# A hybrid decoder block on one core: splitting recurrent outputs where they are made, and moving attention's small work between ScalarE, VectorE and GpSimd

## The chip, the core and the metric

The kernel runs on one core of a Trainium2 chip. The core has TensorE (PE, matrix products; its weight loads are the row PEld), VectorE (DVE), ScalarE (ACT), GpSimd (POOL) and SyncE (SP, which here issues most of the transfers). The metric is the device time in microseconds (us); lower is better.

## The reference

One layer of a decoder block on a sequence of 2048 positions, 1024 wide, in fp32:

```python
h = rms_norm(x, g_norm[l]) * (1.0 + scale) + shift
x_rnn, z_rnn, q, k, v, z_attn, g_r, g_a = split(h @ w_in[l])
xc = causal_depthwise_conv(x_rnn, conv_w[l], conv_b[l])
hr = rg_lru(xc, ...)                       # gated linear recurrence over the positions
y_rnn = (hr * silu(z_rnn)) @ w_out_rnn[l]
o = dilated_attention_mixture(rope(q), rope(k), v)
y_attn = (o * silu(z_attn)) @ w_out_attn[l]
merged = sigmoid(g_r + bg_r) * y_rnn + sigmoid(g_a + bg_a) * y_attn
x = x + gate * (merged @ w_o[l])           # and a last rms_norm
```

The attention has 8 heads of 128. It mixes three causal windows (128 positions at stride 1, 512 at stride 4, 2048 at stride 16), each position weighted by the three softmax denominators.

## The kernel before

**Products in two parts.** Every fp32 operand of a product is split into a high part `h`, which is the number rounded to the type `fp32r` by a copy, and a low part `l`, the rest. A product is then three matmuls (`mm3`: h·h, h·l, l·h). So each operand costs one copy (`hi_act` on ScalarE, or `hi_dve` on VectorE) and one subtraction (`lo_pool` on GpSimd, or `lo_dve` on VectorE).

**Stages.** The positions are worked on in two halves of 1024, each two blocks of 512 columns.

1. For each half the input projection, by Strassen's scheme for 2x2 blocks: seven products of 12 matmuls (`strassen`), whose left operands are made in the first half (and stored as `sD`) and loaded in the second (tile `S`, seven buffers). Among them runs the recurrence: `recurrent` works on 128 channels and two blocks of 512 positions; its steps (taps, split, gates, decay, root, scan, finish) are hung onto the product counter by `steps_after`, so that each runs some products later. `finish` multiplies the recurrent state by its gate, in the tile `zs` (two buffers), and stores it as `yaT`.
2. Attention, 16 heads (8 of the first half, 8 of the second, which have longer key ranges), together with six output products called jobs: the recurrent output product for four blocks (`yaT`, n = 0 to 3) and the attention output product for the first two (`oT`).
3. The other two attention output products and the last projection.

Stages 1 and 3 are ordered by a scheduler from its own cost model. Attention is not: under `manual_schedule` each engine runs its instructions in the order in which the code issues them.

**Attention's order.** A head is six units (`ORDER`): four of strided keys (`c`, 0 to 3; these serve the two dilated windows) and two of local blocks (`w`, 0 and 1). One unit's scores are computed in each slot, the same unit's transposes `LAG` = 7 slots later and its sums one slot after that. In a slot the places are, in order:

- HEAD: high and low parts of keys and queries (`kq`), evictions of the slot before, then the scores on TensorE (`scores_c`, `scores_w`; tile `sc`, two PSUM banks) and their softmax: VectorE adds the mask and takes the extreme (`softmax_tile`, L986), ScalarE the exponential and its sum (L987). The result is `pp`, the statistics are `st`.
- EXCHANGE, once a head (slot e, six after its first): the matmul `exchange` brings the gathered statistics `sm` of the other windows to each position, into an `sc` bank; `maxima`, `exponentials` and then (WEIGHTS) `weights` turn them into the factors `M`.
- The transposes (L1072, L1085; tile `pT`, two banks) and `split_p`, which makes the high and low parts `pth` and `ptl` of a transposed tile.
- TAIL: `scale`, which multiplies the probabilities of the unit whose transposes come in the next slot by `M`; the split of its values (`vh`, `wh`); loads for later slots; and, at the end of slot e - 1, `gather`, which spreads `st` into `sm`.

Between these places `spend` runs 3.6 steps of the jobs per slot, one step being the three matmuls of one k. A job is 64 steps (8 tiles m by 8 k). Its right operands, `yh` and `yl`, are made in the last eight steps of the job before: `load_y` brings `yraw` (four buffers) at steps 44, 46, 48 and 50 and then at each step from 57 on, and `split_y` makes both parts of one k at each step from 56 on. `NY` is the number of buffers of each.

Before the change the lines that matter are: `scale` (L1046 to L1052: VectorE's `tensor_scalar` for `c` at L1049, ScalarE's `activation` for `w` at L1052), `split_p` (L1057), `gather` (L1136, on GpSimd at L1140), `finish` (L678), `load_y` and `split_y` (L1278 and L1285).

Of the kernel before, what the change touches and what calls it, by code (L numbers as in the profile page):

```python
# [10 lines left out]
F32 = mybir.dt.float32  # L11
# [9 lines left out]
P = 128  # L21
S = 2048
D = 1024
# [61 lines left out]
def decoder_block(ctx, tc, x, c, positions, g_norm, w_mod, b_mod, w_in, b_gate, conv_w, conv_b,  # L85
# [10 lines left out]
    def scratch(name, shape):  # L96
        return nc.dram_tensor(name, shape, F32, kind="Internal").ap()
# [5 lines left out]
    zaT = scratch("zaT", [D, S])  # L103
    grT = scratch("grT", [D, S])
    gaT = scratch("gaT", [D, S])
    yaT = scratch("yaT", [D, S])
    mrT = scratch("mrT", [D, S])
    oT = scratch("oT", [D, S])
    meT = scratch("meT", [D, S])
# [42 lines left out]
    def hi_act(o, i):  # L152
        nc.scalar.activation(o, i, AF.Copy)  # L153
# [442 lines left out]
    def recurrent(rp, bigr, f, m):  # L596
# [25 lines left out]
        def x_part(j, ps, u):  # L622
# [55 lines left out]
            def finish():  # L678
                z4 = zs[j][:].rearrange("p (r j) -> p r j", r=4)
                nc.vector.tensor_tensor(z4, v["y"][:].rearrange("p (j r) -> p r j", r=4), z4, ALU.mult)  # L680
                c0 = f * HALF + j * CH
                nc.sync.dma_start(yaT[m * P : (m + 1) * P, c0 : c0 + CH], zs[j][:])

            if j == 0:
                start[0] = n_prod[0]
            steps_after(start[0] + 7 * j, (
                (0, tap), (1, taps), (2, split), (4, gates), (5, sigmoids), (6, decay), (7, exponentials),
                (8, root), (9, scan), (10, finish)))

        def done(i, j, ps, u):  # L690
            (z_part if i else x_part)(j, ps, u)
# [199 lines left out]
    sc = pools.open("sc", bufs=2, space=PSUM)  # L891
    ap_ = pools.open("ap", bufs=1)
    fl = pools.open("fl", side="right", bufs=1)
    NY = 8

    NW = 4
    msk = T(ap_, [P, N_CST - K_M23], F32, "msk")
# [25 lines left out]
    class Head:  # L923
# [121 lines left out]

        def scale(self, kind, x):  # L1046
            for i, pp in enumerate(self.u[kind, x]):
                if kind == "c":
                    nc.vector.tensor_scalar(pp, pp, self.M[:, 0, x, i : i + 1], None, ALU.mult)  # L1049
                else:  # L1050
                    pp = pp[0][:, pp[1] :]
                    nc.scalar.activation(pp, pp, AF.Copy, scale=self.M[:, 1, i, x : x + 1])  # L1052

        def transposes(self, kind, x):
            (self.transposes_c if kind == "c" else self.transposes_w)(x)

        def split_p(self, pt, cols):  # L1057
            th = T(ap_, [P, CH], F32R, "pth", bufs=4)
            tl = T(ap_, [P, CH], F32R, "ptl", bufs=4)
            hi_act(th[:, cols], pt[:, cols])  # L1060
            lo_dve(tl[:, cols], pt[:, cols], th[:, cols])
            return th, tl

        def transposes_c(self, r):
            pp, out = self.u.pop(("c", r)), []
            for k0 in range(0, self.bk[1] + 1, 2):
                pt = T(pT, [P, CH], F32, "pT")
                w = 2 * P + (P if k0 + 1 == self.bk[1] else 2 * P)
                for k in (k0, k0 + 1):
                    c0 = (k % 2) * 2 * P  # L1070
                    for j, i in enumerate([i for i, n in enumerate(self.bk) if n >= k]):
                        nc.tensor.transpose(pt[:, c0 + j * P : c0 + (j + 1) * P], pp[i][:, k * P : (k + 1) * P], ident)  # L1072
                out.append(self.split_p(pt, slice(0, w)))
            self.u["tc", r] = out

        def transposes_w(self, i):

            pt_, out = self.u.pop(("w", i)), []
            for pieces in ((1, 2, 3, 4), (5, 6, 7, 0)):
                pt = T(pT, [P, CH], F32, "pT")  # L1080
                if self.bk[i] == 0 and 0 in pieces:
                    pieces = pieces[:3]
                for c, x in enumerate(pieces):
                    pp, half = pt_[x // 2][0], x % 2
                    nc.tensor.transpose(pt[:, c * P : (c + 1) * P], pp[:, half * P : (half + 1) * P], ident)  # L1085
                out.append(self.split_p(pt, slice(0, len(pieces) * P)))
            self.u["tw", i] = out


# [46 lines left out]
        def gather(self):  # L1136

            self.sm = T(ap_, [P, 2, 4, 2, 8], F32, "sm")
            for g in range(2):
                nc.gpsimd.tensor_tensor(  # L1140
                    self.sm[:, g], self.st[:, :, g].rearrange("p t b n -> p t (b n)").unsqueeze(1).broadcast_to([P, 4, 2, 8]),
                    qm.unsqueeze(2).unsqueeze(3).broadcast_to([P, 4, 2, 8]), ALU.mult)

# [54 lines left out]
        def enlist(self, B):  # L1198
# [3 lines left out]
            for i, s in enumerate((B, B + 2)):  # L1202
                at(s, HEAD, self.window_queries, i)
            e = B + NU
            at(e - 1, TAIL, self.gather)
            at(e, EXCHANGE, self.exchange)
            at(e, EXCHANGE, self.maxima)
            at(e, EXCHANGE, self.exponentials)
# [58 lines left out]
    def steps(jobs):  # L1267
# [4 lines left out]
        def load_w(x):  # L1272

            if x < 2 * len(tiles):
                j, m = tiles[x // 2]
                W[x] = load_wd(jobs[j][0], m, x % 2)

        def load_y(j, k):  # L1278
            if j < len(jobs):
                w, ys, n = jobs[j]  # L1280
                assert ys is yaT or all((n // 2, h, n % 2) in stored for h in range(H))
                t = raw["y", j, k] = T(fl, [P, CH], F32, "yraw", bufs=4)
# [1 line left out]

        def split_y(j, k):  # L1285
            if j < len(jobs):
                t = raw.pop(("y", j, k))
                yh = T(fl, [P, CH], F32R, "yh", bufs=NY)
                yl = T(fl, [P, CH], F32R, "yl", bufs=NY)
                hi_act(yh[:], t[:])  # L1290
                lo_pool(yl[:], t[:], yh[:])
                Y[j, k] = yh, yl

        def load_g(t):
            j, m = tiles[t]
# [28 lines left out]
        for t, (j, m) in enumerate(tiles):  # L1324
            ps = T(pj, [P, CH], F32, "pj")
            for k in range(KT):
# [15 lines left out]
                step = m * KT + k  # L1342
                if step in range(KT * KT - 20, KT * KT - 12, 2):
                    load_y(j + 1, (step - KT * KT + 20) // 2)
                if step >= KT * KT - KT:
                    if k and k + 3 < KT:
                        load_y(j + 1, k + 3)
                    split_y(j + 1, k)
                yield
            last = ps  # L1350
        evict(len(tiles) - 1, last)
# [129 lines left out]
```

## Time and profile before

| | |
|---|---|
| Median of 3 runs | 2396.19 us (2390.61 to 2397.49) |
| Profiled execution: its own time | 2398.24 us |
| Profiled execution: its span | 2396.5 us |
| Busy share of the span: PE, DVE, ACT, POOL | 94%, 58%, 47%, 43% |
| TensorE clock granted over the span | 0.975 |
| Bytes moved | 577.06 MB, 241 GB/s in the mean |
| Attention in the span | about 1503 to 2105 us |

How to read the profile: a row of groups has the line, the engine, the operation, what it writes and reads (out<-in), the shape and the count; behind the bar the time in which it kept the engine busy, the mean duration of one in ns, and the idle time of the engine just before it with what ended it. A row of stages has the stretch, then the busy time of each engine with its instructions, the granted share of TensorE's clock, the mean busy share of the 16 DMA engines and GB/s. A row of waits names who waited for whom, the total, how often, and the longest.

### The profile page before, as it was taken

The page shows a single profiled execution, that of the slowest core. Times are in us where ns is not written, and L with a number is a line of the kernel's source. Part 1 is how long each engine was busy: PE and PEld are TensorE (multiplying, and loading weights), DVE is VectorE, ACT ScalarE, POOL GpSimd, SP SyncE. Part 2 cuts the span into 40 slices and gives each one's busy share as a digit, 9 for nine tenths or more (in the row PEclk, how much of TensorE's full clock was granted, in tenths as well). Part 3 has the DMA queues.
Part 4 walks back from the last instruction along what each step waited for, and adds up shares of the span by engine and source line. Part 5 has one row for each costly group of instructions (what it writes and reads, how often), then busy time and mean ns, then how long its engine had stood idle before and what let it go on. Part 6 is the DMA issues. An engine that isn't in the chain of part 4 may idle for free.

```text
span 2396.5 us, 34064 instructions
## 1 busy us (share of the span) xinstructions
PE 2245.3 (94%) x11397; PEld 1884.5 (79%) x11397; DVE 1392.2 (58%) x2439; ACT 1137.7 (47%) x2268; POOL 1034.0 (43%) x813
## 2 busy tenths in 40 slices
PE   5899999999989999999999998999989898989998
PEld 5897777777777897878888876888878787878887
DVE  6847666766585734443444561477767787845433
ACT  3436656666542525555444411565666666522211
POOL 2566556665554643332211011456565757342000
PEclk9999999999999999999999998999999999999999
DMA  7266877677778559999666776988887678698752
GB/s 264 85 216 216 277 252 263 234 265 252 245 261 267 164 165 330 314 325 294 211 222 224 263 230 228 282 244 261 262 255 240 215 226 253 211 316 278 234 189 97
DMA packets 416295, 577.06 MB, mean 241 GB/s; under 512 B 71934, under 2 KB 278006, under 8 KB 415096
## 3 DMA queue, kind: packets, MB, share of 16 engines
q1 hardware_dynamic: 378680, 455.33, 60.7%
q10 hardware_dynamic: 37440, 119.55, 13.1%
q8 instruction: 90, 1.47, 0.2%
q14 instruction: 85, 0.70, 0.1%
HBM read 362.95 MB, written 211.82 MB: 240 GB/s over the span
## 4 chain that ended last, share of the span: by engine, by line
PE 55%; DMA 10%; DVE 10%; issue 9%; POOL 7%; ACT 5%; SPq 3%; ACTq 1%; POOLq 0%; DVEq 0%
PE pj L145 42%; PE pq L145 7%; PE pg L145 2%; PE sc L145 1%; PE o L145 1%; POOL S L159 1%; DMA wraw<-in_w_in_dram 1%; POOL yl L159 1%; DVE acc L485 1%; DMA wD<-s 1%; POOL vh L159 1%; POOL kq L159 1%; DMA yraw<-yaT 1%; DMA fg<-mrT 1%; DMA vraw<-vN 1%
## 5 line engine op out<-in xcount | busy, mean ns | idle before, releaser
L145 PE MATMUL pj<-T,S 128*128 128x512 f32 x4704 | 1121.5, 398 | 28.6 <-DVE ev L338 17.3
L145 PEld LDWEIGHTS pj<-T,S 128*128 128x128 f32 x4704 | 890.4, 190 | 248.0 <-DVE ev L338 22.5
L145 PE MATMUL pj<-yh,w 128*128 128x512 f32 x1024 | 373.8, 410 | 10.7 <-ACT yh L153 10.7
L159 POOL TENSOR_TENSOR S<-wraw,S 128x512 fp32r<-128x512 f32 x168 | 240.0, 1441 | 176.0 <-ACT S L186 105.0
L145 PEld LDWEIGHTS pj<-yh,w 128*128 128x128 f32 x1024 | 197.6, 193 | 47.8 <-ACT yh L153 11.8
L987 ACT ACTIVATE pp<-pp,st 128x256 f32<-128x256 f32 (+3 forms) x256 | 133.5, 523 | 171.0 <-DVE st L986 171.0
L145 PE MATMUL pj<-yl,w 128*128 128x512 f32 x512 | 205.3, 401 | 2.6 <-POOL yl L159 2.5
L145 PE MATMUL pj<-S,T 128*128 128x256 f32 x1152 | 161.1, 295 | 11.3 <-POOL S L159 7.9
L162 DVE TENSOR_TENSOR ptl<-pT,pth 128x384 fp32r<-128x384 f32 (+1 forms) x160 | 94.8, 626 | 124.6 <-ACT pth L153 124.4
L145 PEld LDWEIGHTS pj<-S,T 128*128 128x128 f32 x1152 | 150.8, 200 | 13.7 <-POOL S L159 9.4
L159 POOL TENSOR_TENSOR S<-s,S 128x512 fp32r<-128x512 f32 x84 | 114.4, 1362 | 91.5 <-ACT S L186 55.3
L159 POOL TENSOR_TENSOR yl<-yraw,yh 128x512 fp32r<-128x512 f32 x64 | 84.8, 1350 | 125.7 <-DMA yraw<-yaT 63.5
L640 DVE SCALAR_TENSOR_TENSOR xc<-xr,par,xc 128x512 f32<-128x512 f32 x96 | 83.5, 870 | 60.5 <-ACT xc L634 57.4
L1049 DVE TENSOR_SCALAR pp<-pp,M 128x128 f32<-128x128 f32 (+3 forms) x128 | 117.3, 956 | 0.0
L159 POOL TENSOR_TENSOR wh<-vraw,wh 128x640 fp32r<-128x640 f32 (+1 forms) x32 | 48.3, 1510 | 159.2 <-ACT wh L153 135.9
L292 DVE TENSOR_TENSOR u<-pj,u 128x512 f32<-128x512 f32 x56 | 38.4, 685 | 134.7 <-PE pj L145 79.5
L145 PEld LDWEIGHTS pj<-yl,w 128*128 128x128 f32 x512 | 99.1, 194 | 19.0 <-POOL yl L159 5.8
L986 DVE CUSTOM_DVE_ANT_0 pp<-sc,msk 128x256 f32<-128x256 f32 (+3 forms) x256 | 102.7, 444 | 16.1 <-PE sc L145 15.7
L159 POOL TENSOR_TENSOR kq<-kraw,kq 128x512 fp32r<-128x512 f32 (+1 forms) x64 | 102.1, 1607 | 13.8 <-ACT kq L153 13.8
L145 PE MATMUL pq<-oh,mh 128*128 128x512 f32 x256 | 98.6, 394 | 8.9 <-ACT mh L153 8.9
L620 POOL TENSOR_TENSOR zs<-zs,sg 128x512 f32<-128x512 f32 x32 | 46.0, 1437 | 133.1 <-ACT sg L616 132.5
L145 PE MATMUL pq<-ol,mh 128*128 128x512 f32 x256 | 100.7, 393 | 0.0
(287 smaller groups left out, 3996.1 us busy)
## 6 DMA issues: line engine op xcount, KB each, us to landing
sD<-S ACTq DMA_DIRECT2D x196, 512.0 KB, 3.4
S<-sD SPq DMA_DIRECT2D x196, 512.0 KB, 5.3
w<-wD SPq DMA_DIRECT2D x128, 512.0 KB, 5.7
wraw<-in_w_in_dram SPq DMA_DIRECT2D x136, 256.0 KB, 3.4
wD<-s ACTq DMA_DIRECT2D x64, 256.0 KB, 4.0
T<-in_w_mod_dram SPq DMA_DIRECT2D x8, 1024.0 KB, 9.6
vN<-ev SPq DMA_DIRECT2D x64, 128.0 KB, 2.3
zaT<-ev SPq DMA_DIRECT2D x32, 256.0 KB, 3.4
```

The costliest lines, as they stand in the source:

```text
L145: last_mm[0] = nc.tensor.matmul(o, lhsT=l, rhs=r, start=st, stop=sp, **kw).ins
L159: nc.gpsimd.tensor_tensor(o, i, h.bitcast(F32), ALU.subtract)
L162: nc.vector.tensor_tensor(o, i, h.bitcast(F32), ALU.subtract)
L292: nc.vector.tensor_tensor(u2[:], Z[:], u1[:], ALU.add)
L485: nc.vector.scalar_tensor_tensor(acc[:], t[:, k, :], ca[:, k : k + 1], acc[:], ALU.mult, ALU.add)
L620: (2, lambda: nc.gpsimd.tensor_tensor(z[:], z[:], sg[0][:], ALU.mult))))
L640: nc.vector.scalar_tensor_tensor(xc, xr[:, i : i + CH], cw(i), xc, ALU.mult, ALU.add)
L986: nc.vector.tensor_tensor_reduce(pdst, s_ps, mask, 1.0, 3e38, ALU.add, ALU.min, m_)
L987: nc.scalar.activation(pdst, pdst, AF.Exp, bias=m_, scale=-1.0, accum_out=l_)
L1049: nc.vector.tensor_scalar(pp, pp, self.M[:, 0, x, i : i + 1], None, ALU.mult)
```

## The change

- In the second half's recurrence one more step, `halves`, splits the finished output: ScalarE makes the high part `yh`, GpSimd the low part, in place in `zs`. The store comes one step later and is two transfers: the low part to `yaT`, the high part to the new `yhT`.
- The jobs on these two blocks (n = 2 and 3; `in_parts`) load `yh` and `yl` ready, with no `yraw` and no split.
- In the other jobs the low part of odd k goes to VectorE. `NY` grows from 8 to 9, and `split_y` runs one step ahead (its first at step 55).
- In attention ScalarE scales the units `c` as well; the high part of a transposed local block is made by VectorE; and `gather` moves from GpSimd at the end of slot e - 1 to VectorE at the head of slot e, in front of the evictions.

```diff
@@ recurrent
             def finish():
                 z4 = zs[j][:].rearrange("p (r j) -> p r j", r=4)
                 nc.vector.tensor_tensor(z4, v["y"][:].rearrange("p (j r) -> p r j", r=4), z4, ALU.mult)
+
+            def halves():
+                if f:
+                    hi_act(new("yh", F32R), zs[j][:])
+                    lo_pool(zs[j][:].bitcast(F32R), zs[j][:], v["yh"][:])
+
+            def store():
                 c0 = f * HALF + j * CH
                 nc.sync.dma_start(yaT[m * P : (m + 1) * P, c0 : c0 + CH], zs[j][:])
+                if f:
+                    nc.sync.dma_start(yhT[m * P : (m + 1) * P, j * CH : (j + 1) * CH], v["yh"][:].bitcast(F32))
...
-                (8, root), (9, scan), (10, finish)))
+                (8, root), (9, scan), (10, finish), (11 if f else 10, halves), (12 if f else 10, store)))
@@ attention
-    NY = 8
+    NY = 9
...
         def scale(self, kind, x):
             for i, pp in enumerate(self.u[kind, x]):
-                if kind == "c":
-                    nc.vector.tensor_scalar(pp, pp, self.M[:, 0, x, i : i + 1], None, ALU.mult)
-                else:
+                if kind == "w":
                     pp = pp[0][:, pp[1] :]
-                    nc.scalar.activation(pp, pp, AF.Copy, scale=self.M[:, 1, i, x : x + 1])
+                w = self.M[:, 0, x, i : i + 1] if kind == "c" else self.M[:, 1, i, x : x + 1]
+                nc.scalar.activation(pp, pp, AF.Copy, scale=w)
...
-        def split_p(self, pt, cols):
+        def split_p(self, pt, cols, hi):
             th = T(ap_, [P, CH], F32R, "pth", bufs=4)
             tl = T(ap_, [P, CH], F32R, "ptl", bufs=4)
-            hi_act(th[:, cols], pt[:, cols])
+            hi(th[:, cols], pt[:, cols])
             lo_dve(tl[:, cols], pt[:, cols], th[:, cols])
             return th, tl
...
-                out.append(self.split_p(pt, slice(0, w)))
+                out.append(self.split_p(pt, slice(0, w), hi_act))
...
-                out.append(self.split_p(pt, slice(0, len(pieces) * P)))
+                out.append(self.split_p(pt, slice(0, len(pieces) * P), hi_dve))
...
-                nc.gpsimd.tensor_tensor(
+                nc.vector.tensor_tensor(
                     self.sm[:, g], self.st[:, :, g].rearrange(...
...
-            at(e - 1, TAIL, self.gather)
+            at(e, HEAD, self.gather)
@@ steps
+        def in_parts(j):
+            return jobs[j][1] is yaT and jobs[j][2] > 1
+
         def load_y(j, k):
-            if j < len(jobs):
+            if j < len(jobs) and not in_parts(j):
...
         def split_y(j, k):
             if j < len(jobs):
-                t = raw.pop(("y", j, k))
-                yh = T(fl, [P, CH], F32R, "yh", bufs=NY)
-                yl = T(fl, [P, CH], F32R, "yl", bufs=NY)
-                hi_act(yh[:], t[:])
-                lo_pool(yl[:], t[:], yh[:])
-                Y[j, k] = yh, yl
+                Y[j, k] = yh, yl = [T(fl, [P, CH], F32R, tag, bufs=NY) for tag in ("yh", "yl")]
+                w, ys, n = jobs[j]
+                rows = slice(k * P, (k + 1) * P)
+                if in_parts(j):
+                    nc.sync.dma_start(yh[:].bitcast(F32), yhT[rows, (n - 2) * CH : (n - 1) * CH])
+                    nc.sync.dma_start(yl[:].bitcast(F32), yaT[rows, n * CH : (n + 1) * CH])
+                else:
+                    t = raw.pop(("y", j, k))
+                    hi_act(yh[:], t[:])
+                    (lo_dve if k % 2 else lo_pool)(yl[:], t[:], yh[:])
...
-                if step >= KT * KT - KT:
-                    if k and k + 3 < KT:
-                        load_y(j + 1, k + 3)
-                    split_y(j + 1, k)
+                if step == KT * KT - KT - 1:
+                    split_y(j + 1, 0)
+                if step >= KT * KT - KT and k + 1 < KT:
+                    if k + 4 < KT:
+                        load_y(j + 1, k + 4)
+                    split_y(j + 1, k + 1)
```

1 line of the change is left out of this document (added).

## The prediction

> **What bounds the kernel now.** I read the span in stages first, then who TensorE waits for in the stage that the change is about, then the groups of that stage, then one wait in order of time. The columns after the length are busy us (instructions) of PE, PEld, DVE, ACT and POOL, then granted clock, DMA share and GB/s.
>
> ```profile
> 1477.00:1503.00 26.00, 12.66 (x31) 7.61 (x31) 1.18 (x2) 6.26 (x10) 11.26 (x9) 0.67 0.79 260
> 1503.00:1795.00 292.00, 274.55 (x1683) 241.46 (x1682) 191.57 (x569) 182.43 (x538) 172.85 (x182) 0.98 0.86 259
> 1795.00:2105.00 310.00, 288.83 (x1794) 253.52 (x1793) 239.67 (x531) 190.63 (x477) 176.94 (x146) 0.98 0.74 229
> 2105.00:2397.00 292.00, 274.15 (x1203) 225.99 (x1201) 124.48 (x205) 56.83 (x89) 45.94 (x25) 0.97 0.66 223
> ```
>
> Attention (1503 to 2105, heads of the first half to about 1795, of the second behind it) keeps TensorE 94% busy. VectorE is the next busiest, 66% and then 77%. So the stage is TensorE's work plus short gaps. Who ends the gaps of PE there (us, times, longest):
>
> ```profile
> PE sc L145 <- POOL sm L1140: 14.0, 4, 5.5
> PE sc L145 <- DVE st L986: 10.6, 6, 3.7
> PE pT L1072 <- DVE pp L1049: 10.3, 12, 1.4
> PE pT L1085 <- ACT pp L1052: 2.5, 1, 2.5
> PE sc L145 <- POOL q L948: 0.9, 2, 0.5
> ```
>
> The first two rows are one place: the exchange matmul, once a head. It needs the gathered statistics (POOL) and a score bank that VectorE's softmax must have read. Rows three and four are transposes that wait for scaled probabilities. The groups (busy, mean ns | idle before):
>
> ```profile
> L987 ACT ACTIVATE pp<-pp,st 128x512 f32<-128x512 f32 x32 | 22.9, 714 | 0.0
> L1049 DVE TENSOR_SCALAR pp<-pp,M 128x384 f32<-128x384 f32 x32 | 37.6, 1176 | 0.0
> L1049 DVE TENSOR_SCALAR pp<-pp,M 128x512 f32<-128x512 f32 x32 | 35.2, 1099 | 0.0
> L1308 DVE TENSOR_TENSOR fg<-fg,fg 128x512 f32<-128x512 f32 x14 | 12.4, 887 | 0.5
> ```
>
> The 384-wide scale costs more than the 512-wide one, so it isn't its size that is paid for. One exchange in order of time (start, us):
>
> ```profile
> 1868.31 1.46 POOL L159 TENSOR_TENSOR vh<-vraw,vh 128x512 fp32r<-128x512 f32 x1
> 1869.71 0.55 POOL L1140 TENSOR_TENSOR sm<-st,cs 128x64 f32<-128x64 f32 x2
> ...
> 1867.14 1.48 DVE L1049 TENSOR_SCALAR pp<-pp,M 128x512 f32<-128x512 f32 x1
> 1868.55 0.68 DVE L1131 TENSOR_TENSOR yw<-o,zt 128x512 f32<-128x512 f32 x1
> 1869.15 0.54 DVE L986 CUSTOM_DVE_ANT_0 pp<-sc,msk 128x384 f32<-128x384 f32 x1
> ...
> 1879.18 0.80 DVE L1049 TENSOR_SCALAR pp<-pp,M 128x384 f32<-128x384 f32 x2
> ...
> 1870.32 0.49 PE L145 MATMUL sc<-sm,msk 128*128 128x128 f32 x2 [3.73 <-DVE st L986]
> ...
> 1870.30:1875.10 4.80, 4.78 (x22) 4.33 (x23) 3.87 (x9) 3.26 (x10) 4.80 (x5) 0.65 0.43 127
> ```
>
> At 1867 a scale takes 1.48 us under a busy POOL; at 1879, with POOL idle, both scales of a unit take 0.80 together. Instructions that read PSUM (yw, softmax) keep 0.68 and 0.54 whatever POOL does. VectorE falls behind, POOL's gather stands behind its queue of low parts, and TensorE idles 3.73 us. The last line is the stage row behind that gap: clock 0.65. The trace's clock records hold seven stretches at half speed between 1503 and 2105, one of 6.83 and six of 3.41 us. Some 3.3 of these 27.3 us lie inside the gaps themselves, so half of the other 24.0, 12.0 us, is lost on top.
>
> **The change part by part.** The sum is against the profiled execution, 2398.2 us (span 2396.5 and 1.7 around it); the median of the runs shown is 2396.2, 2.0 below.
>
> *Scales of the dilated units to ScalarE.* VectorE loses 128 instructions, 117.3 us (page: mean 956 ns). ScalarE gains 32 each of 128, 256, 384 and 512 columns, by its own rows of these widths 0.40, 0.50, 0.61 and 0.71: 71 us. The 12 gaps before the transposes (10.3) have VectorE's lateness as their cause and go; what is late next is ScalarE, which scales behind its high parts and, for a head's first unit, behind the weights. Queued behind that scale are a value split and the next exponentials; the latter wait for VectorE anyway (171.0 us over the stage). Of 12.8 us I leave 6: two or three waits like the one 2.5 us gap that ScalarE causes now, at job boundaries where its high parts wait for loads. Bounds 0 and 12.8 plus what the second rival takes.
>
> *High parts of local blocks to VectorE.* ScalarE loses 64 (56 by 0.584, 8 by 0.475: 36 us). No row shows this copy; it reads PSUM as ptl does (0.69 at 512) and as the rotary sign does (0.75): 44 us on VectorE. ptl then waits for nothing but its own engine. Hidden: the sums are one slot (about 5.8 us) later.
>
> *Gather to VectorE, from the end of one slot to the head of the next.* It leaves POOL's queue (10.7 us in 32). On VectorE it stands ahead of the eviction and of the softmax that frees the bank. Its inputs lie in SBUF: small operations of this kind (L1163, L1164) took 0.17 with POOL idle and up to 1.32 beside it, so 0.34 to 2.6 a head, against 0.8 to 2.9 of scales that go from the same stretch. It waits for ScalarE's exponentials of the slot before, done before the ptl ahead of it. Of 24.6 us I leave 8, 0.5 a head. Bounds 0 (no gap) and 24.6 (all stay); more than that, up to the gather's own 2.6 a head, only if the scales had not left the same stretch.
>
> *Odd low parts to VectorE.* Jobs 1, 4, 5: 12 by 0.69 to 1.7 (L1308's extremes); POOL loses 12 by 1.30. In order behind ScalarE's high part, which can wait 3.3 us for a load: inside what I left above. VectorE's sum: -117 +44 +12 (gathers at 0.4) +12 = -49 of 431; POOL -36 -11 of 350; ScalarE +71 -36 -10 = +25 of 373.
>
> *Jobs 2 and 3 read ready parts.* No split: 16 high and 16 low parts less. But 16 loads of 256 KB instead of 8 are issued, and in the last 8 or 9 steps instead of 20. A step is about 1.6 us (384 from 1486 to 2105): 4.2 MB in 13 us, 325 GB/s beside the stage's 259, where the best slices of the page move 330. So some 10 us of backlog. On SP each pair waits for TensorE's last read of the slot, and key, value, gate and weight loads stand behind; TensorE gets there unhindered. A part is needed 9 steps (14.5 us) after its issue, against 5.7 to landing plus 10. On the edge: I take 2 us, bounds -2 and +16.
>
> *Transition (1477 to 1503).* Low parts alternate, so raw buffers come free 1.9 us earlier (the last load's wait was for POOL's fourth low part, and VectorE does that one 0.6 behind its high part) and the last low part takes 0.7 instead of 1.3: -2.6, bounds 0 and -4. VectorE is idle there.
>
> *Second-half recurrence.* Added: 16 high parts (0.62, ScalarE 42% busy), 16 low parts (1.4, POOL 16% busy from 1100 on), 16 stores of 256 KB; stores move one or two products later. TensorE is 100% busy from 1100 to 1430 on operands loaded up to seven products (2.8 us each) ahead. Without that cover: SP waits for a low part with loads behind it; a z buffer is held 5.6 us longer, which delays a write after blocks 0 and 4 by up to 4 us each; and from 910 to 1100 (DMA share 0.95, 323 GB/s) about 2.1 MB cost 6.5 us. Bounds 0 and 14; I take 1, nearest to the full cover.
>
> *Clock.* With fewer gaps, seven slow stretches become about three: 12.0 to 5.4, -6.6, bounds 0 and -12.
>
> *Tail.* Same work, slightly other order: 0, bounds -3 and +3.
>
> Sum: -16.6 -6.8 +2 -2.6 +1 -6.6 = -29.6, so 2368.6 on the profiled execution and 2366.6 against the median: **2367**.
>
> [...]
>
> **Rivals.** *The exchange keeps its gaps.* Six of the ten end with the softmax that frees the bank, and VectorE still has eviction, gather and softmax in that stretch. For: the small operations reach 1.32 beside POOL. Against: some 2 us of scales vanish ahead of it. Left are -6.8, -2.6 and +3: 2390, no measurable change (0.3% of this kernel, 7 us, is what can be told).
>
> *The burst binds.* Gates and values arrive late at both boundaries, 8 us each with 1.7 of slow clock: 17 us of the gain go, 2384. For: the backlog above. Against: share 0.97 at 1520 to 1540 left no gap in PE.
>
> *ScalarE takes VectorE's place* (the other side). In the slots of local softmax it has four exponentials (0.49 apart with their reads), two high parts, four scales and a value split, 5.1 us of 5.8. If transposes of the 64 dilated units wait 0.9 us each for it, 58 us replace the 6 I left: +22, 2418. It decides against the change from 0.67 us a unit. For: the 2.5 us gap at 2019. Against: these slots gain nothing, the scale falls in the others, and ScalarE idles 171 us for VectorE. [...]
>
> **Numbers.** Forecast 0.66 (own range 2350 to 2382), burst 0.14, gaps stay 0.08, ScalarE 0.12. Faster 0.80, same 0.08, slower 0.12. The range 2348 to 2394 leaves out ScalarE's case and some 0.07 at its edges.
>
> **What would show it.** Right: PE's gaps before the exchange below 10 us and none ended by POOL, before transposes below 7, clock 0.99 from 1503 on, VectorE under 70% and ScalarE about 70% there. Wrong: more than 20 us of gaps ended by ScalarE's scale or, near the second and third job boundary, by gate or value loads; TensorE no longer full before 1430.

## The result, and the profile after

The changed kernel takes 2358.64 us (median of 4 runs, 2354.15 to 2364.77) where the kernel before, in 4 runs beside it, takes 2394.61. The ratio is 0.985, with a 95% interval of 0.982 to 0.9885. The forecast was 2367, in a range of 2348 to 2394. The profiled execution is the longest of the four: 2364.8 us, span 2363.0, against a span of 2396.5 before.

The stages of the span first. The columns are those of before: the stretch, its length, busy us (instructions) of PE, PEld, DVE, ACT and POOL, granted clock, DMA share, GB/s.

```profile
1480.00:1506.00 26.00, 13.93 (x40) 8.49 (x39) 4.65 (x6) 5.04 (x8) 5.09 (x4) 0.74 0.79 245
1506.00:1790.00 284.00, 275.43 (x1707) 242.91 (x1706) 174.12 (x567) 185.87 (x560) 145.19 (x144) 0.99 0.92 280
1790.00:2085.00 295.00, 290.77 (x1837) 259.42 (x1835) 207.96 (x518) 215.93 (x511) 167.28 (x129) 0.99 0.84 256
2085.00:2363.00 278.00, 260.93 (x1138) 214.82 (x1137) 119.34 (x200) 53.32 (x84) 37.97 (x19) 0.98 0.65 221
```

Attention now keeps TensorE 98% busy (566 of 579 us from 1506 to 2085) where it was 94%. Over these rows VectorE's busy share is 66% and ScalarE's 69%. The waits of PE in attention (us in total, times, longest):

```profile
PE sc L147 <- DVE sm L1150: 5.2, 1, 5.2
PE sc L147 <- DVE st L997: 2.2, 2, 1.9
PE sc L147 <- POOL q L959: 1.5, 1, 1.5
PE pj L147 <- ACT yh L155: 1.4, 1, 1.4
PE pT L1082 <- DVE ptl L164: 1.1, 2, 0.7
PE pT L1082 <- ACT pp L1062: 0.8, 2, 0.6
PE pj L147 <- DMA yh<-yhT: 0.8, 2, 0.4
PE pj L147 <- DMA yl<-yaT: 0.5, 2, 0.3
```

The exchange waits 7.5 us in all instead of 24.6, and in three heads instead of ten; the transposes 2.0 instead of 12.8. The ready parts are waited for 1.5, with the waits that are too short for a row; the 1.4 us for `yh` belong to the transition into attention. Groups of attention (line, engine, operation, tiles, shape and count | busy us, mean ns | idle before):

```profile
L1062 ACT ACTIVATE pp<-pp,M 128x512 f32<-128x512 f32 x32 | 22.8, 713 | 0.0
L1062 ACT ACTIVATE pp<-pp,M 128x384 f32<-128x384 f32 x32 | 19.5, 609 | 5.2 <-DVE M L1186 5.2
L158 DVE CAST pth<-pT 128x512 fp32r<-128x512 f32 x56 | 38.4, 685 | 30.8 <-PE pT L1095 30.8
L1150 DVE TENSOR_TENSOR sm<-st,cs 128x64 f32<-128x64 f32 x32 | 9.4, 334 | 0.7 <-ACT pp L998 0.7
```

On ScalarE the two wide scales cost 713 and 609 ns, against 1099 and 1176 on VectorE before. The copy that had no row takes 0.69 us, as `ptl` does.

Where the 33.5 us of the two spans lie: the first matmul of the jobs comes 5.3 us later (1491.8, before 1486.5); from it to the first matmul of the last projection 601.2 us instead of 640.3, -39.1; behind that +0.4.

### The profile page after: what moved, and what is told of

The parts are those of the page before. It is cut to its first block, busy times and chain, and to the rows that moved or that the text cites. A ratio compares the mean times of both kernels' runs of the same rounds, so it can differ in the third digit from the quotient of the medians.

```text
span 2363.0 us, 34030 instructions
## 1 busy us (share of the span) xinstructions
PE 2232.6 (94%) x11397; PEld 1877.8 (79%) x11397; DVE 1340.2 (57%) x2423; ACT 1170.4 (50%) x2332; POOL 1003.8 (42%) x765
## 4 chain that ended last, share of the span: by engine, by line
PE 61%; DMA 12%; DVE 11%; ACT 5%; issue 5%; POOL 3%; SPq 2%; ACTq 1%; DVEq 0%; POOLq 0%
PE pj L147 43%; PE pq L147 7%; PE o L147 3%; PE sc L147 3%; PE pg L147 2%; DMA wraw<-in_w_in_dram 2%; POOL S L161 1%; PE pT L1082 1%; DMA w<-wD 1%; DVE acc L487 1%; DMA wD<-s 1%; ACT S L188 1%; DMA kraw<-qT 1%; PE pT L1095 1%; DMA qT<-t 1%
## 5 line engine op out<-in xcount | busy, mean ns | idle before, releaser
L147 PE MATMUL pj<-T,S 128*128 128x512 f32 x4704 | 1119.5, 398 | 33.7 <-DVE ev L340 15.7
L147 PEld LDWEIGHTS pj<-yh,w 128*128 128x128 f32 x1024 | 195.6, 191 | 50.3 <-ACT yh L155 12.5
L164 DVE TENSOR_TENSOR ptl<-pT,pth 128x384 fp32r<-128x384 f32 (+1 forms) x160 | 97.8, 628 | 60.8 <-ACT pth L155 58.6
L1062 ACT ACTIVATE pp<-pp,M 128x256 f32<-128x256 f32 (+3 forms) x256 | 118.0, 523 | 12.7 <-DVE M L1186 12.7
L997 DVE CUSTOM_DVE_ANT_0 pp<-sc,msk 128x256 f32<-128x256 f32 (+3 forms) x256 | 105.2, 449 | 24.6 <-PE sc L147 21.4
L161 POOL TENSOR_TENSOR vh<-vraw,vh 128x256 fp32r<-128x256 f32 (+1 forms) x64 | 66.4, 1037 | 94.8 <-ACT vh L155 83.1
L147 PE MATMUL pq<-oh,ml 128*128 128x512 f32 x256 | 99.6, 390 | 0.0
```

The source lines that it names most:

```text
L147: last_mm[0] = nc.tensor.matmul(o, lhsT=l, rhs=r, start=st, stop=sp, **kw).ins
L161: nc.gpsimd.tensor_tensor(o, i, h.bitcast(F32), ALU.subtract)
L164: nc.vector.tensor_tensor(o, i, h.bitcast(F32), ALU.subtract)
L997: nc.vector.tensor_tensor_reduce(pdst, s_ps, mask, 1.0, 3e38, ALU.add, ALU.min, m_)
L1062: nc.scalar.activation(pp, pp, AF.Copy, scale=w)
```

## The experiments

All ratios are to the kernel before, run beside each kernel on the same chip, with 95% intervals. The middle columns are from one profiled execution each: time from the first matmul of the jobs to the first of the last projection, gaps of PE in attention before the exchange and before transposes, and time at half clock in attention (us).

| kernel | ratio | jobs and attention | exchange | transposes | half clock |
|---|---|---|---|---|---|
| before | 1 | 640.3 | 24.6 | 12.8 | 27.3 |
| changed | 0.9853 (0.982 to 0.9885) | 601.2 | 7.5 | 2.0 | 13.7 |
| before, scales on ScalarE | 0.9893 (0.9872 to 0.9915) | 610.4 | 16.8 | 3.1 | 20.5 |
| before, gather on VectorE | 1.0100 (1.0081 to 1.0119) | 661.2 | 41.9 | 10.5 | 47.8 |
| before, both of these | 0.9878 (0.9859 to 0.9897) | 606.7 | 9.3 | 5.9 | 17.1 |
| before, ready parts | 1.0001 (0.9987 to 1.0015) | 633.5 | 22.7 | 11.9 | 17.1 |
| before, recurrence's work only | 1.0024 (1.0013 to 1.0034) | 635.0 | 24.1 | 10.0 | 30.7 |
| changed, gather on POOL | 0.9921 (0.9906 to 0.9935) | 608.1 | 11.9 | 4.4 | 10.2 |
| changed, no ready parts | 0.9879 (0.9856 to 0.9901) | 605.1 | 14.4 | 3.5 | 17.1 |
| changed, all low parts on POOL | 0.9881 (0.9866 to 0.9896) | 605.4 | 4.3 | 3.7 | 10.2 |
| changed, copies on ScalarE | 0.9849 (0.9831 to 0.9867) | 594.3 | 5.2 | 1.8 | 6.8 |
| changed, work moved to ScalarE doubled | 0.9891 (0.9874 to 0.9907) | 611.9 | 5.8 | 8.9 | 13.7 |
| changed, job 1 ready too | 1.0000 (0.9988 to 1.0013) | 608.5 | 2.5 | 5.2 | 10.2 |
| changed, no ready parts, six raw buffers | 0.9843 (0.9823 to 0.9863) | 601.2 | 9.1 | 3.7 | 13.7 |

One execution's column is good to some 5 us: the kernel before and the one with the recurrence's work only run the same attention and differ by 5.3.

### The scales alone

```diff
-                if kind == "c":
-                    nc.vector.tensor_scalar(pp, pp, self.M[:, 0, x, i : i + 1], None, ALU.mult)
-                else:
-                    pp = pp[0][:, pp[1] :]
-                    nc.scalar.activation(pp, pp, AF.Copy, scale=self.M[:, 1, i, x : x + 1])
+                if kind == "w":
+                    pp = pp[0][:, pp[1] :]
+                w = self.M[:, 0, x, i : i + 1] if kind == "c" else self.M[:, 1, i, x : x + 1]
+                nc.scalar.activation(pp, pp, AF.Copy, scale=w)
```

> The kernel before with one part of the change: ScalarE scales the dilated units. Theory A (VectorE's scales, stretched to 1.1 us beside a busy POOL, are what makes both the softmax of the exchange and the transposes late): the gaps before the transposes fall from 12.8 us to below 7, those before the exchange from 24.6 to about 12 (the ones that POOL's gather ends stay in part), half clock in attention falls from 27 us to about 14; some 22 to 25 us faster than before, 2371. Rival B (the gather in POOL's queue is the cause): only the gaps before the transposes go, 7 us and a little clock, 2386. Rival C (ScalarE takes VectorE's place): gaps before transposes ended by ScalarE's scale, over 20 us, not faster than before.

Measured: 0.9893, some 26 us faster. The waits of PE for the exchange and the transposes in this kernel:

```profile
PE sc L145 <- POOL sm L1139: 16.8, 6, 5.1
PE pT L1084 <- ACT pp L1051: 1.7, 1, 1.7
PE pT L1071 <- ACT pp L1051: 1.2, 2, 1.0
```

No gap ends with VectorE any more, neither before a transpose nor before the exchange: its scales had been behind both. What is left of the exchange's gaps are six waits for POOL's gather. Theory A holds for the time and the causes; it had put the rest of the exchange at 12 us rather than 16.8 and half clock at 14 rather than 20.5. Rival C is out: ScalarE ends 2.9 us of gaps.

### The gather alone

```diff
-                nc.gpsimd.tensor_tensor(
+                nc.vector.tensor_tensor(
...
-            at(e - 1, TAIL, self.gather)
+            at(e, HEAD, self.gather)
```

> The kernel before with one part of the change: the gather on VectorE, at the head of the next slot. Theory A: the gaps that POOL ends (14.0 us) go, but VectorE still has its 1.1 us scales in that stretch and the gather on top, so the gaps that VectorE ends grow from 10.6 to about 20: within 5 us of before, 2390 to 2396. Rival B: the gaps before the exchange fall to 10 us and the half clock with them, 18 to 20 us faster, 2376.

Measured: 1.0100, 24 us slower. Both theories were too kind to it: A had allowed 5 us. The waits of PE for VectorE in attention and then one exchange in order of time (start, us, engine, line, operation, tiles and shape, count, and in brackets the idle time before):

```profile
PE sc L145 <- DVE st L986: 32.7, 8, 5.2
PE sc L145 <- DVE sm L1140: 9.2, 7, 3.3
PE pT L1072 <- DVE pp L1049: 7.7, 10, 1.0
```

```profile
1876.02 2.16 DVE L1049 TENSOR_SCALAR pp<-pp,M 128x384 f32<-128x384 f32 x2
1877.86 1.44 POOL L159 TENSOR_TENSOR vh<-vraw,vh 128x512 fp32r<-128x512 f32 x1
1878.10 3.03 DVE L1140 TENSOR_TENSOR sm<-st,cs 128x64 f32<-128x64 f32 x2
1879.26 1.80 POOL L159 TENSOR_TENSOR kq<-kraw,kq 128x768 fp32r<-128x768 f32 x1
1881.06 0.68 DVE L1131 TENSOR_TENSOR yw<-o,zt 128x512 f32<-128x512 f32 x1
1881.66 0.54 DVE L986 CUSTOM_DVE_ANT_0 pp<-sc,msk 128x384 f32<-128x384 f32 x1
1882.13 0.68 DVE L986 CUSTOM_DVE_ANT_0 pp<-sc,msk 128x512 f32<-128x512 f32 x1
1882.26 0.80 PE L145 MATMUL sc<-sm,msk 128*128 128x128 f32 x2 [5.23 <-DVE st L986]
```

POOL's gather no longer ends a gap, but fifteen of the sixteen exchanges wait for VectorE. In the queue ahead of the softmax that frees the bank stand two stretched scales (2.16 us), then the gather, which is itself stretched to 3.03 us for two instructions of 64 columns, then the eviction. The gather's 3.03 us lie beside POOL's low parts of `vh` and `kq`. In the changed kernel its 27 instructions that run with POOL idle take 215 to 226 ns each, the four that lie beside POOL's work from end to end 791 to 1329. `yw` and the softmax, which read PSUM, keep their 0.68 and 0.54 right behind the gather, beside POOL's copies of `q`. The 32 `yw` of this kernel take 683 ns in the mean; in the kernel before, 14 with POOL idle take 679 to 692, and 14 that lie wholly beside its low parts and gathers 676 to 692. Why the gather gives way there and `yw` does not isn't shown.

### Both

The two edits above together.

> The kernel before with two parts of the change: ScalarE scales the dilated units, and the gather is on VectorE at the head of the next slot. Alone, the first gave a ratio of 0.989 and the second 1.010. Theory A (one queue: the gather on VectorE costs only as long as the scales, stretched beside POOL, stand in the same stretch): the exchange gaps fall to 8 to 12 us, attention is as short as with all parts but for job boundaries; ratio 0.985 to 0.988. Rival E (the two add up, and copy, odd low parts and ready parts make the rest of the gain): ratio 0.997 to 1.002.

PE's waits for the exchange in this kernel, the row above 0.3 us:

```profile
PE sc L145 <- DVE st L986: 9.0, 2, 8.3
```

Measured: 0.9878, in theory A's range. One edit loses 24 us alone; on top of the other it loses nothing that can be measured. The two do not add up, because they share a queue: rival E is out. Nearly all of what the exchange still waits is one gap of 8.3 us at 1753, at a job boundary.

### The changed kernel with the gather back on POOL

```diff
-                nc.vector.tensor_tensor(
+                nc.gpsimd.tensor_tensor(
...
-            at(e, HEAD, self.gather)
+            at(e - 1, TAIL, self.gather)
```

> The changed kernel with the gather back on POOL at the end of the slot. Theory A: at the boundaries of jobs with raw blocks POOL's gather again stands behind low parts, though half of these are now VectorE's: POOL ends gaps of 4 to 8 us in place of VectorE's 7, and half clock stays at 14 to 20 us; 0 to 6 us slower than the changed kernel, ratio to the kernel before 0.985 to 0.988. Rival B (the gather's move is a large part of the gain): gaps ended by POOL of 15 us or more, 12 us or more slower, ratio 0.990 or above.

PE's waits for the exchange in this kernel:

```profile
PE sc L147 <- POOL sm L1150: 11.8, 5, 6.6
```

Measured: 0.9921, 0.7% or 16 us behind the changed kernel, in rival B's range. But rival B's 15 us of gaps aren't there: POOL ends 11.8. The profiled executions differ by 6.9 us in jobs and attention and by 4.6 us ahead of them, where the two programs have the same instructions. So the timed 16 us is larger than the 6.9 that the profile shows where the edit acts. A part of the remainder is in the choice of executions: the profiled one of the changed kernel is 6.1 us above that kernel's median, the one of this kernel is its median. The rest is open.

### Ready parts alone, and the changed kernel without them

The first is the kernel before with the recurrence's two parts, their loads and the splits one step earlier; the second takes just these parts out of the changed kernel:

```diff
-            return jobs[j][1] is yaT and jobs[j][2] > 1
+            return False
...
-                if f:
+                if False:
                     hi_act(new("yh", F32R), zs[j][:])
```

> The kernel before with one part of the change: the recurrence writes high and low parts of the second half, jobs 2 and 3 load them, and the splits are placed as in the changed kernel. Theory A: PE reaches the jobs some 5 us later (1492 instead of 1486.5), as in the changed kernel; in jobs 2 and 3 POOL has 16 low parts less, so scales are stretched less and some 6 to 10 us of gaps go: within 5 us of before, 2388 to 2396. Rival D (it is POOL's relief in these jobs that unstretches VectorE): 15 us or more of gaps and clock go, 2383 or less.

> The changed kernel without the recurrence's parts: jobs 2 and 3 load raw blocks and split them as the others do. Theory A: PE reaches the jobs at about 1486.5, as before, 5 us earlier than in the changed kernel; jobs 2 and 3 get waits for raw loads and low parts at their boundaries, 3 to 5 us: the same time as the changed kernel within 5 us, 2355 to 2362. Rival D: the stretched low parts come back in jobs 2 and 3, 12 us or more of gaps and clock, 2368 or more.

Measured: 1.0001, and 0.9879 where the changed kernel has 0.9853; the intervals of the last two overlap. Alone the ready parts are worth nothing; within the change they may be worth 6 us, which isn't settled. Both theories missed in part. Without the parts theory A expected the changed kernel's time and the jobs 5 us earlier; they start at 1492.4, no earlier than in the changed kernel (1491.8), and by the ratio the time (2366 beside the 2394.6 above) lies between the two theories. With the parts alone the jobs start at 1497.0, not 1492, and the gaps before exchange and transposes shrink by 2.8 us, not 6 to 10: POOL has 16 low parts less, which relieves it at two boundaries only, and over attention VectorE's scales still take 905 ns in the mean, before 956. In jobs 2 and 3 they do what they should: without them the exchange waits for VectorE at 1661 (3.0 us) and 1759 (3.8 us) as well, with them 1.5 us of load waits stand there. Rival D is out for the ready parts alone. So no run here keeps the scales on VectorE and takes most of the stretch away; that they delayed the exchange by being stretched, and not by their number alone, is read from the rows.

### The recurrence's work alone

```diff
+            def halves():
+                if f:
+                    hi_act(new("yh", F32R), zs[j][:])
+                    lo_pool(zs[j][:].bitcast(F32R), zs[j][:], v["yh"][:])
+
             def store():
...
+                if f:
+                    nc.sync.dma_start(yhT[m * P : (m + 1) * P, j * CH : (j + 1) * CH], v["yh"][:].bitcast(F32))
...
-                (8, root), (9, scan), (10, finish)))
+                (8, root), (9, scan), (10, finish), (11 if f else 10, halves), (12 if f else 10, store)))
```

> The kernel before, with the recurrence's high and low parts and their 16 more stores in the second half, as the changed kernel has them; every job still loads the outputs as before and splits them itself (its low parts are of what now is a low part, so the product of jobs 2 and 3 leaves out the high parts). Theory A: from the attention of the kernel with all of the parts' edits 6.8 us shorter at the same time, the recurrence costs 5 to 7 us, by later loads at the end of the recurrent products: ratio 1.002 to 1.003. Rival F (it is covered, and the late loads near 1440 are what executions differ by anyway): ratio 0.999 to 1.001.

Measured: 1.0024 (1.0013 to 1.0034), that is 5.7 us, 3.1 to 8.1. The product of jobs 2 and 3 leaves out the high parts here; the jobs run as many instructions as before. PE's wait for a left operand from 1400 to 1480, before and then with this work:

```profile
PE pj L145 <- DMA S<-sD: 0.7, 1, 0.7
```

```profile
PE pj L146 <- DMA S<-sD: 5.2, 1, 5.2
```

The wait for a left operand is 4.9 to 5.3 us in each of the eight kernels that do this work, and 0.7 to 2.3 in the six that don't. In the changed kernel SP issues those loads from 1438 on, behind a run of `qT` and `kT` stores that starts at 1430; in the kernel before such loads stand between the stores. SP's rows, the changed kernel and then the one before:

```profile
1429.97 3.96 SPq L801 DMA_DIRECT2D qT<-t  x6
1434.03 4.02 SPq L801 DMA_DIRECT2D kT<-t  x6
1440.13 15.05 SPq L269 DMA_DIRECT2D S<-sD  x10
```

```profile
1427.51 3.24 SPq L790 DMA_DIRECT2D qT<-t  x5
1430.85 1.03 SPq L267 DMA_DIRECT2D S<-sD  x2
1431.97 1.17 SPq L790 DMA_DIRECT2D kT<-t  x2
```

The work itself lies elsewhere; what it does is change the order in which the scheduler deals out SP's queue. In return the wait of 2.9 to 3.4 us near 1065 of the kernels without this work is 0 to 2.6 us with it. The theory's place holds, and its size by the timed runs; in the two profiles TensorE's waits from 905 to 1480 grow by 3.5 us in sum, and the jobs start 3.6 us later. But the profiled start of the jobs scatters by 11.5 us among kernels that are alike up to there (1486.5 to 1498.0), so the time is told by the timed runs alone.

### Job 1 ready too

```diff
-                if f:
+                if f or j:
                     hi_act(new("yh", F32R), zs[j][:])
...
-            return jobs[j][1] is yaT and jobs[j][2] > 1
+            return jobs[j][1] is yaT and jobs[j][2] > 0
```

> The changed kernel with the block of job 1 as ready parts too: 8 high parts, 8 low parts and 8 stores more in the first half's recurrence, and no split at the boundary of jobs 0 and 1. Theory A (what is left of the exchange gaps there comes from ScalarE waiting for raw blocks, and VectorE behind it): the gap of 5.2 us near 1567 and the half clock of 6.8 us behind it go, in place of waits for loads of 1 us; the first half pays 0 to 3 us: 5 to 8 us faster than the changed kernel, ratio to the kernel before 0.982 to 0.983. Rival G (16 loads in that boundary, beside value and key loads, are late): gaps before the products of job 1 of 5 us or more, no gain, 0.985 or above.

Measured: 1.0000: the whole gain is gone. The exchange's gaps fall to 2.5 us, as theory A had it. The loss lies far ahead, where the jobs start at 1516.6 instead of 1491.8. Matmuls that the changed and this kernel get done from 300 to 600 and 600 to 900, changed kernel first:

```profile
300.00:600.00 300.00, 283.49 (x1199) 225.46 (x1198) 195.12 (x211) 183.40 (x301) 180.71 (x130) 0.99 0.73 254
600.00:900.00 300.00, 276.86 (x1562) 239.68 (x1561) 177.13 (x263) 125.97 (x216) 163.83 (x115) 0.97 0.70 219
```

```profile
300.00:600.00 300.00, 278.29 (x1152) 219.42 (x1151) 186.04 (x205) 179.43 (x296) 181.53 (x130) 0.98 0.72 247
600.00:900.00 300.00, 272.26 (x1477) 232.23 (x1477) 186.91 (x269) 129.74 (x223) 164.99 (x117) 0.97 0.69 215
```

It gets 47 and then 85 fewer done. From 200 to 900 TensorE's waits for evictions grow from 15.7 to 18.4 us, those for `xh` from 3.3 to 6.2, and a new one of 4.4 for a statistic of the norm appears, 10 us in sum. Time at half clock there grows from 27.3 to 41.0 us, of which about half, 7 us, is lost (an estimate from the granted clock). Together that is nearly the 17.5 us by which the 4000th matmul of the trace starts later (886.9, changed kernel 869.4). The rest of the 24.8 us arises behind it, and I can't name it. Sixteen pairs of parts cost 5.7 us in the second half, eight cost four times that in the first, where POOL is 60% busy (181 of 300 us) and not 20%; that POOL's load is the reason isn't shown.

### All low parts on POOL, and the copies back on ScalarE

```diff
-                    (lo_dve if k % 2 else lo_pool)(yl[:], t[:], yh[:])
+                    lo_pool(yl[:], t[:], yh[:])
```

> The changed kernel with all low parts of job blocks on POOL. Theory A: jobs 1, 4 and 5 get four more low parts of 1.3 us each at their boundaries and the transition four in a row: 2 us at the transition, 1 to 3 us at the boundaries, 2 to 5 us slower than the changed kernel, ratio to the kernel before 0.986 to 0.988. Rival: VectorE in turn keeps up with the softmax at these boundaries, and the gap of 5.2 us near 1567 goes: ratio 0.982 to 0.984.

Measured: 0.9881, 6.7 us behind the changed kernel, with overlapping intervals. The profile doesn't say that VectorE's odd low parts help the exchange: without them its gaps are 4.3 us, less than 7.5, and the one near 1567 is 2.8 us instead of 5.2, towards what the rival had expected. Nor does the transition take the 2 us more of theory A: the first tile of job 0 is done in 13.1 us, in the changed kernel in 13.7. So the time is near theory A's and its reasons aren't there.

```diff
-                out.append(self.split_p(pt, slice(0, len(pieces) * P), hi_dve))
+                out.append(self.split_p(pt, slice(0, len(pieces) * P), hi_act))
```

> The changed kernel with the high parts of local blocks back on ScalarE: 36 us more on ScalarE, 44 less on VectorE, in slots where both have about 5 of 5.8 us. Theory A (neither binds): within 4 us of the changed kernel, ratio to the kernel before 0.984 to 0.987. Rival C (ScalarE is near its bound): transposes and local scales wait for ScalarE, 10 us or more slower, ratio 0.989 or above.

Measured: 0.9849, the changed kernel's time. Which of the two engines makes these 64 copies makes no difference; neither binds.

### The work moved to ScalarE, doubled

```diff
+                if kind == "c":
+                    nc.scalar.activation(pp, pp, AF.Copy)
                 nc.scalar.activation(pp, pp, AF.Copy, scale=w)
```

> The changed kernel with every scale of a dilated unit preceded by a copy of the same size in place on ScalarE: the work that was moved to ScalarE, doubled (128 more instructions, some 71 us). Theory A (ScalarE has room: its exponentials still wait 88.7 us for VectorE): transposes wait in some units only, 5 to 15 us slower than the changed kernel, ratio to the kernel before 0.987 to 0.992. Rival C (ScalarE takes VectorE's place): the transposes of the 64 dilated units wait 0.7 us and more each, 45 us or more with the clock, ratio 1.0 or above.

Measured: 0.9891, some 9 us behind the changed kernel, with overlapping intervals. Its waits for transposes:

```profile
PE pT L1084 <- ACT pp L1064: 7.6, 9, 1.6
PE pT L1097 <- ACT pp L1064: 0.6, 1, 0.6
```

Each dilated unit has 0.92 us more on ScalarE (58.6 us in 128 copies), and TensorE waits for a scale ten times, 8.2 us in all: a seventh of what was added. ScalarE has room left; rival C would have needed 0.67 us of waiting in every one of the 64 units.

### Six raw buffers

```diff
-    NY = 9
+    NY = 8
...
-                t = raw["y", j, k] = T(fl, [P, CH], F32, "yraw", bufs=4)
+                t = raw["y", j, k] = T(fl, [P, CH], F32, "yraw", bufs=6)
...
-                if step in range(KT * KT - 20, KT * KT - 12, 2):
+                if step in range(KT * KT - 24, KT * KT - 12, 2):
```

The recurrence's parts are taken out as above, and `split_y` starts at step 56 again. This was to be better than both the changed kernel and the one without parts. The reason why it should be is in the changed kernel's largest gap, in order of time:

```profile
1563.52 0.63 ACT L155 ACTIVATE yh<-yraw 128x512 fp32r<-128x512 f32 x1 [2.96 <-DMA yraw<-yaT]
1564.05 0.47 ACT L155 ACTIVATE pth<-pT 128x384 fp32r<-128x384 f32 x1
1564.56 0.56 DVE L164 TENSOR_TENSOR ptl<-pT,pth 128x384 fp32r<-128x384 f32 x1 [2.62 <-ACT pth L155]
1565.86 0.63 ACT L155 ACTIVATE yh<-yraw 128x512 fp32r<-128x512 f32 x1 [1.34 <-DMA yraw<-yaT]
1566.58 0.69 DVE L164 TENSOR_TENSOR yl<-yraw,yh 128x512 fp32r<-128x512 f32 x1 [1.47 <-ACT yh L155]
1567.19 0.35 DVE L1150 TENSOR_TENSOR sm<-st,cs 128x64 f32<-128x64 f32 x2
1567.60 0.80 PE L147 MATMUL sc<-sm,msk 128*128 128x128 f32 x2 [5.23 <-DVE sm L1150]
```

ScalarE waits for a raw block, `ptl` and the odd low part for ScalarE, the gather for these, TensorE for the gather: one late load runs through three queues.

> The changed kernel without the recurrence's parts, with six buffers of raw blocks instead of four (paid for by eight pairs of part buffers instead of nine), so that six of a job's eight loads are issued ahead of its first split. Theory A (the gaps left at boundaries of raw jobs come from ScalarE waiting 3 us and more for the fifth block on, and VectorE behind it; the recurrence's stores cost 5.7 us): with raw blocks on time, the exchange gaps at 1567, 1661 and 1759 (12.5 us in the kernel without parts) and the half clock behind them (13.7 us) shrink to a third, and the recurrence costs nothing: 5 to 10 us faster than the changed kernel, ratio to the kernel before 0.981 to 0.984. Rival H (these gaps are VectorE's and POOL's low parts, not the loads): gaps as without parts, ratio 0.986 to 0.989.

Measured: 0.9843, no different from the changed kernel. The loads come in time: ScalarE waits for none at that boundary, and the first tile of job 0 is done in 9.4 us, against 13.7 in the changed kernel and 14.3 before. But the gap stays, 3.8 us, with another cause:

```profile
1556.46 3.38 DVE L164 TENSOR_TENSOR yl<-yraw,yh 128x512 fp32r<-128x512 f32 x2
1559.76 0.55 DVE L164 TENSOR_TENSOR ptl<-pT,pth 128x384 fp32r<-128x384 f32 x1
1560.23 1.50 DVE L1150 TENSOR_TENSOR sm<-st,cs 128x64 f32<-128x64 f32 x2
1561.79 0.80 PE L147 MATMUL sc<-sm,msk 128*128 128x128 f32 x2 [3.83 <-DVE sm L1150]
```

Two low parts now come back to back on VectorE, beside POOL's, and take 1.69 us each where one with POOL idle took 0.69; then the gather takes 1.50 beside POOL's `vh` and `kq` instead of 0.35. The gaps at 1562, 1657 and 1753 are 8.9 us in sum, where the kernel without parts has 12.5 and theory A had expected a third of that. Theory A is right on the loads and the transition and wrong on the gaps, which are rival H's. No kernel of this study beats the changed one by more than can be measured.

## Why the prediction was right

The direction, the place and the mechanism held: VectorE's queue was what TensorE waited for, and taking the scales, stretched beside POOL (1099 and 1176 ns for the wide ones), out of it is most of the gain (26 of 35 us alone). Step by step, us, by the two profiled executions unless said otherwise:

| step | forecast | measured |
|---|---|---|
| exchange gaps | -16.6 | -17.1 |
| transposes | -6.8 | -10.8 |
| ready parts' loads | +2 | +1.5 |
| transition | -2.6 | -0.7 |
| recurrence | +1 | +5.3; timed alone +5.7 |
| clock | -6.6 | -7.7 |
| tail | 0 | +0.4 |
| sum | -29.6 | -33.5 (span) |

The measured terms add up to -29.1, but that this is so near the forecast is luck: terms that gained up to 4.0 us more than forecast (transposes, clock) and terms that cost up to 4.3 us more (recurrence, transition) cancel. The other 4.4 us of the span are delays under 0.1 us between matmuls, some 2 by a count of start-to-start times, and what two executions differ by. The signs that I had named came as forecast: exchange gaps below 10 us with none ended by POOL, transposes below 7, clock 0.99, VectorE at 66% and ScalarE at 69%.

- **Exchange.** The forecast left 8 us and 7.5 are left. Its condition was the important part: the gather costs more on VectorE "only if the scales had not left the same stretch". The gather alone shows that case: gaps grow by 17.3 us, 1.1 a head, within the bound of 2.6 a head, though one head's gather reached 3.0.
- **Transposes.** I left 6 us for ScalarE being late at job boundaries; 2.0 are left, 0.8 of them ScalarE's. With ready parts in jobs 2 and 3 there is nothing to be late for there.
- **Copies.** Costed at nothing, and moving them back changes nothing.
- **Odd low parts.** Put "inside what I left above". That is so in size; the one 5.2 us gap left has an odd low part in its chain.
- **Transition.** This step failed: 0.7 us instead of 2.6. It had said that "raw buffers come free 1.9 us earlier". The last load was issued 5.1 us behind the first matmul of the jobs, before 5.5: only 0.4 earlier, since the fourth low part, now VectorE's, took 1.19 us beside POOL and not the 0.7 that I had used. That load then landed later (6.6 us to the split, before 5.8), which ate the gain. One pair of profiles is a weak basis here: the same first tile of job 0 takes 12.4 to 14.3 us in the five kernels with the old splits and 11.2 to 13.7 in the six with alternating ones, 12.9 and 12.0 in the mean. The gain of the means, 0.9 us, is still far below 2.6. Six raw buffers, in the last experiment, brought the tile to 9.4 us, below all of these, so the buffers were the right suspect and alternating low parts too weak a remedy.
- **Recurrence.** This term was too small, 1 against 5.7 (3.1 to 8.1), within its bounds of 0 and 14. I had looked for the cost where the work lies, from 910 to 1430 under a busy TensorE. It appears at 1440, behind it, where a reordered SP queue issues the left operands late. "TensorE no longer full before 1430" was the sign I had named, and TensorE was 99.7% busy there.
- **Clock.** Half clock in attention fell from 27.3 to 13.7 us, in three stretches, the number forecast. By start-to-start times of the matmuls the seven stretches cost 11.6 us before (forecast from 12.0) and the three cost 5.0 now (5.4): -6.6, as forecast. The other 1.1 us is the end of an eighth stretch, from 1499.6 to 1503 and behind the first tile, which the forecast had not counted.
- **Rivals.** "The exchange keeps its gaps" and "the burst binds" are excluded by the rows above (7.5 us at the exchange; 1.5 us for the ready parts, and none for gates or values). "ScalarE takes VectorE's place" is excluded with its work doubled.

## What to carry to other kernels

Ask of an instruction that moves to another engine's queue what stands ahead of it there at that moment, and move the slow neighbours first: the same edit lost 24 us alone and nothing once the scales had left. VectorE, 66 and 77% busy in attention, still made TensorE wait in the kernel before, with scales stretched beside POOL (512 columns took 1099 ns in the mean and 473 to 476 in the seven that ran with POOL idle); compare the mean of one form with its duration in a stretch where the other engine is idle. Work added under a full TensorE was still paid for later here, 5.7 us, by the order that the scheduler gave to SP's queue.

## What the runs showed of the hardware

**Where the granted clock changed.** In all 14 profiled executions the granted clock changes only on a grid of 3.413 us. I counted TensorE's idle time (from the modelled end of one matmul to the start of the next, all gaps) in each window of this grid from 1040 to 2080 us and looked at the clock of the next window:

```
idle in a window at full clock   windows   next window at half clock
under 1.39 us                    4011      0
1.39 to 1.83 us                  29        7
1.83 us and more                 80        80
idle in a window at half clock   windows   next window at half clock
under 0.3 us                     79        0
0.3 to 0.6 us                    9         2
0.6 us and more                  61        61
```

In these executions half clock followed the idle sum of the window before it (1.83 of 3.41 us and more: 80 of 80 windows; under 1.39: none of 4011) and not the length of a gap. A gap of 1.46 us (1788, the changed kernel) that fell into one window with little else was followed by half clock; one of 2.92 us (1064.5, the kernel before) that was split into 1.16 and 1.76 over two windows was not.

**Executions of the same instructions differ ahead of attention.** In six kernels whose engines run the same instructions in the same order up to 1400 us and that do the same work up to the jobs, these start between 1486.5 and 1498.0 us. A cost of a few us there can't be read from one profile.
